# Half-group input projections with 512-row products, and the time mixing's gate projected ahead of the keys

## The chip, the cores and the metric

The kernel runs on one core of a Trainium2 chip. The metric is the device time of one execution in microseconds (us). TensorE (PE) multiplies matrices into PSUM; VectorE (DVE), ScalarE (ACT) and GpSimd (POOL) work on tiles in SBUF and PSUM; SyncE (SP) issues most of the loads. Each engine runs its own list of instructions in order, and waits where an instruction needs a result that is not there yet.

## What is computed

Two decoder layers over 256 tokens of width 2048. Each layer makes one input projection, gives its columns to three token mixers, gates each mixer's output, joins the three and projects them back:

```python
for l in range(DEPTH):
    u = x @ w_in[l]
    (cb, cc, ch, cg, cq, ckv, kpe, mg, rcols, rg) = _split(u, IN_SIZES)
    y_conv = _short_conv_branch(cb, cc, ch, cg, conv_w[l])
    y_mla = _mla_branch(cq, ckv, kpe, mg, ...)
    y_rwkv = _rwkv7_branch(rcols, rg, ...)
    mix = jnp.concatenate([y_conv, y_mla, y_rwkv], axis=-1)
    x = _layer_norm(DEEPNORM_ALPHA * x + mix @ w_out[l], ln_g[l], ln_b[l])
```

The convolution branch is `cb * conv3(cc * ch) * silu(cg)`. The attention branch norms `cq` and `ckv`, projects queries from the one and keys and values from the other, attends with 8 heads, and multiplies with `silu(mg)`. The time mixing (RWKV-7) runs a recurrence over the tokens with 8 heads of 64, norms its output by head (a group norm), adds a bonus term, and multiplies with `silu(rg)`.

## The kernel before

All products keep full precision by splitting both factors in a high and a low part (float32r): `hi` is a rounded copy made on ScalarE, `lo` the rest, made by a subtraction on VectorE (`split_in`). A product of two such factors is three TensorE products (`mm3`, lines 331 to 334): high by high, high by low, low by high.

The input projection is done in 12 groups of 512 columns. `in_group` computes one: for each of 16 blocks of 128 of the 2048 input rows, and each of 4 blocks of 128 columns, `mm3` multiplies a 128x128 block of weights with the 256 tokens of x. That makes 64 triples of 256-row products a group. The result lies in two accumulators of one PSUM bank each (`u_NAME_0`, `u_NAME_1`; pool `pp`, 4 buffers), and the work behind reads it there. Weights come as loads of 1 MB on SP's queue (`load`, three buffers in pool `wr`, asked for one load ahead by `LOOK`), and are split on ScalarE and VectorE in steps of 1024 columns into `hi_NAME` and `lo_NAME` (four buffers each).

The order of the groups is k, r, a, v, cq, cc, ch, cb, cg (`MAIN`), then the keys and values (`mla_kv`, products pkn and pvt in four rounds) and queries (`mla_q`, pqn and pqp) of the attention, and then rg, mg0, mg1 (`LATE`). rg is the gate of the time mixing, mg0 and mg1 are the gates of the attention.

The other work of a layer is written as generators (`rwkv`, `latent`, `conv`) that are advanced by `tick()` between the groups' steps. The order of each engine's list is then set by a scheduler, which weighs priorities (`tc.high_priority`) and when it believes each instruction can start.

The time mixing works in four chunks of 64 tokens. `pg` holds products within a chunk, made of `ar` and of `bk`; half of `bk` is written by POOL (lines 565 and 572). `bd`, `bt`, `xi` and the steps `tm` invert a triangular matrix on VectorE; `xd` and `xq` are moves of the result through DMA, and `pz` and `px` finish it. Then comes the serial part. For each chunk c, `prh_c` applies the state to the chunk's inputs, `rhs` adds `qs`, `pu_c` multiplies by the inverse and is copied to `uvt` (one half on VectorE, one on ScalarE), `pst_c` and two VectorE operations make the next state `st_c`, and after every second chunk `py_0`, `py_1` give the output. `py` is copied to `y`, normed by head (`gm`, `gsq`, `gv`, `grs` and the small steps `nr_g`), turned by `pt` into `yy`, and with the bonus `bon` and the gate (`th_rg`) becomes `mr`, a factor of the output projection. `mc` is that of the convolution, and `ma0`, `ma1` those of the attention.

The keys and values leave PSUM by copies of ScalarE into `kn` and `vt`, and a split into `vs`. These tiles, like `mc`, `mr`, `ma` and others, take turns in slots of the pool `sl`. The output projection (`out_proj`, products po) uses 512-row products, with the weights as the moving factor.

Of the kernel before, what the change touches and what calls it, by code (L numbers as in the profile page):

```python
# [10 lines left out]
F32 = mybir.dt.float32  # L11
# [13 lines left out]
AHEAD = 1500  # L25
GATE = 'V'
OFF = 2
LOOK = 1
# [3 lines left out]
N8 = 9  # L32
HEADS = 8
# [50 lines left out]
def lay_out(inp):  # L84
# [3 lines left out]
    w = inp["w_in"][:, :, idx].reshape(L, NKC, P, len(GROUPS), 512)  # L88
    o = {"x": inp["x"], "positions": inp["positions"]}
    o["xT"] = inp["x"][0].T.reshape(NKC, P, S).transpose(1, 0, 2)  # L90
    o["w_in"] = w.transpose(0, 3, 2, 1, 4)
# [18 lines left out]
def hybrid_layers(ctx: ExitStack, tc: tile.TileContext, x, positions, xT, w_in, w_out, w_uq, w_ukv, par, wa_in, gb_in,  # L110
# [189 lines left out]
    def split_w(raw, name, behind, to):  # L300
        nk, n = raw.shape[1:]
        k = 1024 // n if n == 256 else 2
        hi, lo = to or [wh.tile([P, k, 1024 // k], F32R, tag=t, name=f"{t}_{name}") for t in ("hi", "lo")]
        with tc.high_priority(AHEAD):
            ops = split_in(hi[:, 0:nk, 0:n], lo[:, 0:nk, 0:n], raw)
# [36 lines left out]
    MAIN, LATE, ORDER = ("k", "r", "a", "v", "cq", "cc", "ch", "cb", "cg"), ("rg", "mg0", "mg1"), (0, 12, 4, 8)  # L342

    def plan():

        for l in range(L):
            for names in (MAIN, None, LATE):
                if names is None:
                    yield from ((f"ukv{l}_{i}", 0, 2, w_ukv[l, i]) for i in range(4))
                    yield from ((f"uq{l}_{i}", 0, 4, w_uq[l, i]) for i in range(4))  # L350
                for name in names or ():
                    first = l == 0 and name == GROUPS[0]
                    for k0, nk in STEPS if first else [(k, 4) for k in (0, 4, 8, 12)]:
                        yield f"{name}{l}", k0, nk, w_in[l, GROUPS.index(name)]
            for g in range(3):
                yield from ((f"wo{l}_{g}", k0, 4, w_out[l, g]) for k0 in ORDER)
# [3 lines left out]
    loads, ready, asked = plan(), {}, []  # L360

    def load():
# [4 lines left out]
        n = src.shape[2]  # L367
        raw = to = behind = None
        if name == "k0":
            load_x(k0, nk)  # L370
            raw = s4(f"w_first{k0}", (P, nk, 512)) if k0 < 10 else None
        elif name[0] == "k":
            behind = mark.get(int(name[1])) if k0 else None
        elif name == f"wo{L - 1}_3_0" or name[0] == "w" and name[2] != str(L - 1) and name[3:] == "_3_1" and k0:
            s = s8(f"wl{name}_{k0}", (P, 2, 4, 256), F32R)
            to = s[:, 0], s[:, 1]
        if raw is None:
            raw = wr.tile([P, 4, n] if n < 512 else [P, 4, 512], F32, tag="raw", name=f"w_{name}_{k0}")
        i = nc.sync.dma_start(raw[:, 0:nk], src[:, k0:k0 + nk, :])
        if not params:  # L380
            in_turn(1, i)
        d = 4 if n == 256 else 2
        ready[name, k0] = [(k0 + k, split_w(raw[:, k:min(k + d, nk)], f"{name}_{k0}_{k}",
                                            behind and k0 + k > 2 and behind[k0 + k > 4], to))
                           for k in range(0, nk, d)]
# [6 lines left out]

    def in_group(l, xs, name):
        ps = [pp.tile([P, 2, S], F32, tag="acc", name=f"u_{name}{l}_{i}") for i in range(2)]
        first = l == 0 and name == GROUPS[0]
        if first:
            warm_up()
        for k0, step in STEPS if first else [(k, 4) for k in (0, 4, 8, 12)]:
            for k2, (hi, lo) in weights(f"{name}{l}", k0):
                for kc in range(k2, min(k2 + 2, k0 + step)):  # L400
                    k = kc - k2
                    for b in range(4):
                        mm3(ps[b // 2][:, b % 2, :], hi[:, k, b * P:(b + 1) * P], lo[:, k, b * P:(b + 1) * P],
                            *hl(xs, kc), kc == 0 and b % 2 == 0, kc == NKC - 1)
# [944 lines left out]
```

## Time and profile before

| | |
|---|---|
| median of 3 runs | 933.12 us (930.76 to 933.73) |
| profiled execution | 930.57 us |
| its span, first to last instruction | 928.8 us |
| granted TensorE clock, mean | 0.996 |
| products on TensorE | 7719 |

The profile lists how long each engine was busy, and how often an engine stood idle and whose result ended that. Views used below are the page of the whole execution; the waits of an engine (total, times, longest); the timeline (start and duration of each instruction, in us from the start of the span); the groups of instructions by tile (least, median and longest duration in ns, first and last start); and windows, which give for each stretch its length and the busy time and number of instructions of PE, PEld (weight loads), DVE, ACT and POOL, then the granted TensorE clock, the DMA share and GB/s. Where products follow each other on TensorE, the distance of their starts is the time that they take; the durations in the rows are longer, since products overlap.

### The profile page before, as it was taken

How to read it: one execution, taken by the hardware profiler on the slowest of the kernel's cores; microseconds unless marked ns; L12 is line 12 of the kernel's file. 1: busy time of each engine (PE TensorE's matmuls, PEld its weight loads, DVE VectorE, ACT ScalarE, POOL GpSimd, SP SyncE). 2: the span in 40 equal slices, each digit the busy share in tenths (PEclk: the TensorE clock that was granted, in tenths of full speed). 3: DMA queues.
4: the chain of work that ended last, by engine and by line, in shares of the span. 5: the costliest groups of instructions: out<-in, count | busy, mean ns of one | idle time of the engine just before them, and what ended most of it. 6: DMA issues, size and time to landing. Idle time of an engine off the chain costs nothing.

```text
span 928.8 us, 18409 instructions
## 1 busy us (share of the span) xinstructions
PE 910.0 (98%) x7719; PEld 867.6 (93%) x7719; DVE 682.1 (73%) x1132; ACT 468.2 (50%) x716; POOL 42.0 (5%) x47
## 2 busy tenths in 40 slices
PE   8999999999999999999999999999999999999996
PEld 7999989999989999888899999899998999998895
DVE  6687898886569875666766688988854898755665
ACT  6656535543455675434346465463434657754430
POOL 1210130000000000000010001300000000000000
PEclk9999999999999999999999999999999999999999
DMA  8965355354425435964665544463544363259542
GB/s 295 288 200 181 137 187 165 127 183 137 163 98 188 176 127 170 345 208 149 204 227 182 178 148 175 148 203 136 183 117 137 135 225 141 97 175 371 177 136 90
DMA packets 47523, 165.12 MB, mean 178 GB/s; under 512 B 13446, under 2 KB 22198, under 8 KB 32582
## 3 DMA queue, kind: packets, MB, share of 16 engines
q1 hardware_dynamic: 39680, 150.35, 47.4%
q10 hardware_dynamic: 5072, 9.57, 3.3%
q0 software_dynamic: 2688, 4.03, 1.6%
q8 instruction: 60, 0.98, 0.4%
q14 instruction: 23, 0.19, 0.1%
HBM read 158.61 MB, written 5.32 MB: 177 GB/s over the span
## 4 chain that ended last, share of the span: by engine, by line
PE 89%; DMA 3%; DVE 3%; POOL 2%; ACT 1%; issue 1%; SPq 0%; DVEq 0%; ACTq 0%
PE po L332 6%; PE po L333 6%; PE po L334 6%; PE u_mg L334 3%; PE u_mg L333 3%; PE u_mg L332 3%; PE u_ch L332 2%; PE u_cg L333 2%; PE u_cc L332 2%; PE u_cg L332 2%; POOL bk L572 2%; PE u_cg L334 2%; PE u_rg L334 2%; PE u_rg L333 2%; PE u_rg L332 2%; PE u_cb L334 2%
## 5 line engine op out<-in xcount | busy, mean ns | idle before, releaser
L136 DVE TENSOR_TENSOR lo_wo<-w_wo,hi_wo 128x1024 fp32r<-128x1024 f32 x57 | 69.4, 1223 | 51.7 <-ACT hi_wo L136 50.3
L136 ACT CAST hi_wo<-w_wo 128x1024 fp32r<-128x1024 f32 x57 | 59.8, 1053 | 80.8 <-PE po L334 56.0
L333 PE MATMUL u_mg<-x,hi_mg 128*128 128x256 f32 x256 | 72.6, 283 | 0.0
L334 PE MATMUL u_mg<-x,lo_mg 128*128 128x256 f32 x256 | 72.6, 283 | 0.0
L332 PE MATMUL u_mg<-x,hi_mg 128*128 128x256 f32 x256 | 72.4, 283 | 0.0
L136 DVE TENSOR_TENSOR lo_mg<-w_mg,hi_mg 128x1024 fp32r<-128x1024 f32 x32 | 39.1, 1223 | 18.5 <-ACT hi_mg L136 18.4
L333 PEld LDWEIGHTS u_mg<-x,hi_mg 128*128 128x128 f32 x256 | 49.1, 192 | 0.0
L334 PEld LDWEIGHTS u_mg<-x,lo_mg 128*128 128x128 f32 x256 | 49.0, 192 | 0.0
L332 PEld LDWEIGHTS u_mg<-x,hi_mg 128*128 128x128 f32 x256 | 49.0, 192 | 0.0
L333 PE MATMUL po<-lo_wo,ma 128*128 128x512 f32 (+1 forms) x128 | 46.4, 362 | 0.0
L334 PE MATMUL po<-hi_wo,ma 128*128 128x512 f32 (+1 forms) x128 | 46.4, 362 | 0.0
L332 PE MATMUL po<-hi_wo,ma 128*128 128x512 f32 (+1 forms) x128 | 45.9, 363 | 0.0
L136 ACT CAST hi_mg<-w_mg 128x1024 fp32r<-128x1024 f32 x32 | 33.6, 1049 | 22.1 <-PE u_mg L333 13.3
L332 PE MATMUL u_ch<-x,hi_ch 128*128 128x256 f32 x128 | 37.0, 289 | 0.0
L333 PE MATMUL u_cg<-x,hi_cg 128*128 128x256 f32 x128 | 37.0, 289 | 0.0
L334 PE MATMUL u_cq<-x,lo_cq 128*128 128x256 f32 x128 | 37.0, 289 | 0.0
L332 PE MATMUL u_k<-x,hi_k 128*128 128x256 f32 x128 | 36.5, 290 | 0.4 <-ACT hi_k L136 0.3
L333 PE MATMUL u_cq<-x,hi_cq 128*128 128x256 f32 x128 | 36.7, 287 | 0.0
L332 PE MATMUL u_cc<-x,hi_cc 128*128 128x256 f32 x128 | 36.7, 289 | 0.0
L332 PE MATMUL u_cq<-x,hi_cq 128*128 128x256 f32 x128 | 36.6, 286 | 0.0
L332 PE MATMUL u_cg<-x,hi_cg 128*128 128x256 f32 x128 | 36.6, 286 | 0.0
L334 PE MATMUL u_k<-x,lo_k 128*128 128x256 f32 x128 | 35.6, 285 | 0.9 <-DVE lo_k L136 0.9
(424 smaller groups left out, 3417.2 us busy)
## 6 DMA issues: line engine op xcount, KB each, us to landing
w_wo<-in_w_out_dram SPq DMA_DIRECT2D x24, 1024.0 KB, 6.1
w_mg<-in_w_in_dram SPq DMA_DIRECT2D x16, 1024.0 KB, 4.8
w_r<-in_w_in_dram SPq DMA_DIRECT2D x8, 1024.0 KB, 6.4
w_a<-in_w_in_dram SPq DMA_DIRECT2D x8, 1024.0 KB, 4.9
w_v<-in_w_in_dram SPq DMA_DIRECT2D x8, 1024.0 KB, 4.9
w_cq<-in_w_in_dram SPq DMA_DIRECT2D x8, 1024.0 KB, 4.8
w_cc<-in_w_in_dram SPq DMA_DIRECT2D x8, 1024.0 KB, 4.9
w_ch<-in_w_in_dram SPq DMA_DIRECT2D x8, 1024.0 KB, 5.2
```

Of the source, the lines that this page charges most:

```text
L136: inst = call(*args, **kwargs)
L332: m = T.matmul(o, lh, rh, start=first, stop=False, skip_group_check=True)
L333: T.matmul(o, lh, rl, start=False, stop=False, skip_group_check=True)
L334: T.matmul(o, ll, rh, start=False, stop=last, skip_group_check=True)
L572: G.tensor_tensor(bk[hi_, :, 64:128], c16(kkn)[hi_], c16(pinv)[hi_], ALU.mult)
```

## The change

Five things change together.

1. All groups but k are computed in two half-groups of 256 columns. One product of a weights' high part with 512 rows (x high and x low side by side) replaces two products of 256, and one product of the low part with x high follows. The two halves of the sums lie side by side in an accumulator of two banks (`acc`, 2 buffers instead of 4 of one bank). On the way out ScalarE copies the one half to SBUF and VectorE adds the other, into `u2_NAME` (in the instruction lists printed as `u_NAME`, with a number), or into `ccc`, `ccq`, `ckv` for the groups whose copies in SBUF were made separately before. k keeps its three 256-row products (`wide_group`).
2. Loads are of 0.5 MB instead of 1 MB, five buffers of half the size, asked for two ahead.
3. rg moves from `LATE` to the end of `MAIN`, ahead of keys and queries. The tiles of keys and values of a round share one accumulator (`pkv`), those of the queries too (`pq`), and their way out has a higher priority (`EVICT`).
4. POOL's two passes over `bk` become eight chunks, and `pg` of a chunk waits for its own chunks alone.
5. The first product of several small steps is given all the waits of the step (`gather`), and their two halves are taken in the other order.

```diff
-LOOK = 1
+EVICT = 4000
+LOOK = 2
...
-    pp = ctx.enter_context(tc.tile_pool(name="pp", bufs=4, space=PSUM))
+    pp = ctx.enter_context(tc.tile_pool(name="pp", bufs=2, space=PSUM))
...
-    wr = ctx.enter_context(tc.tile_pool(name="wr", bufs=3))
+    wr = ctx.enter_context(tc.tile_pool(name="wr", bufs=5))
...
+    def gather(m, earlier):
+
+        for e in earlier:
+            after(m, e)
...
-    MAIN, LATE, ORDER = ("k", "r", "a", "v", "cq", "cc", "ch", "cb", "cg"), ("rg", "mg0", "mg1"), (0, 12, 4, 8)
+    MAIN, LATE, ORDER = ("k", "r", "a", "v", "cq", "cc", "ch", "cb", "cg", "rg"), ("mg0", "mg1"), (0, 12, 4, 8)
+
+    def acc(name):
+
+        return pp.tile([P, 2, 512], F32, tag="acc", name=name)
...
+        whole = c4(f"c{name}{l}") if name in ("cc", "cq") else None
+        pairs = []
+        for i in range(2):
+            ps = acc(f"u_{name}{l}_{i}")
+            for k0 in range(0, NKC, 4):
+                _, (hi, lo) = weights(f"{name}{l}_{i}", k0)
+                for k in range(4):
+                    x2 = xs[k0 // 4][:, :, k, :]
+                    for b in range(2):
+                        c = slice(b * P, b * P + P)
+                        T.matmul(ps[:, b, :].rearrange("p (i t) -> p i t", i=2), hi[:, k, c], x2, start=k0 + k == 0,
+                                 stop=False, skip_group_check=True)
+                        T.matmul(ps[:, b, 0:S], lo[:, k, c], x2[:, 0, :], start=False, stop=k0 + k == NKC - 1,
+                                 skip_group_check=True)
...
+            with tc.high_priority(AHEAD):
+                A.copy(to, ps[:, :, S:2 * S])
+                V.tensor_tensor(to, to, ps[:, :, 0:S], ALU.add)
...
-        G.tensor_tensor(bk[hi_, :, 64:128], c16(kkn)[hi_], c16(pinv)[hi_], ALU.mult)
+        ready_ = []
+        for c in range(4):
+            if c == 2:
+                chunk(3, kp, 0)
+            ready_.append([chunk(c, kkn, 64)])
...
-            pk = pp.tile([P, 2, S], F32, tag="acc", name=f"pkn{l}_{h2}")
-            pv = pp.tile([P, 2, S], F32, tag="acc", name=f"pvt{l}_{h2}")
+            pk, pv = (t.rearrange("p (b c) -> p b c", b=2) for t in (lambda a: (a[:, 0], a[:, 1]))(acc(f"pkv{l}_{h2}")))
...
-            with tc.high_priority(AHEAD):
+            with tc.high_priority(EVICT):
```

TensorE's list at the end of layer 0's recurrence, before the change; names as above, with buffer numbers behind them. First the place of pu_2, then that of pst_2:

```order
1942 L333 MATMUL pkn_3_3250<-hkv_1647,hi_ukv_3_0_0_3203 128x256
1943 L334 MATMUL pkn_3_3250<-hkv_1647,lo_ukv_3_0_0_3204 128x256
1944 L774 MATMUL pu_2_2921<-rhs_2_2885,xq_2409 64x64 x8
1945 L332 MATMUL pvt_3_3251<-hi_ukv_3_0_0_3203,hkv_1647 128x256
1946 L333 MATMUL pvt_3_3251<-lo_ukv_3_0_0_3204,hkv_1647 128x256
```

Large products of keys and values (12 of pvt_3) stand between pu_2 and pst_2; 19 of pqn_0 follow prh_3 in the same way, and pt comes only in the group mg0. After the change, at the same step:

```order
1519 L338 MATMUL pkv_1_2986<-lo_ukv_1_0_2895,hkv_1434 128x256
1520 L339 MATMUL pkv_1_2986<-hi_ukv_1_0_2894,hkv_1434 128x256
1521 L843 MATMUL pu_2_2531<-rhs_2_2506,xq_2091 64x64 x8
1522 L859 MATMUL pst_2_2564<-uvt_1678,bkt_1609 64x64 x8
1523 L836 MATMUL prh_3_2598<-st_2_2573,ar_1156 64x64 x8
1524 L843 MATMUL pu_3_2634<-rhs_3_2607,xq_2091 64x64 x8
1525 L812 MATMUL py_1_0_2645<-uvt_1678,gs_1_1290 64x64 x8
```

The steps of the last two chunks stand one behind the other. A little further on, where py_1 ends:

```order
1542 L821 MATMUL py_1_1_2646<-st_1_2441,ar_1156 64x64
1543 L821 MATMUL py_1_1_2646<-st_2_2573,ar_1156 64x64
1544 L902 MATMUL pt_0_2809<-cs,y_2318 128x128 x4
1545 L902 MATMUL pt_1_2840<-cs,y_2318 128x128 x4
1546 L337 MATMUL pkv_2_3021<-hkv_1434,hi_ukv_2_0_2941 128x256
```

pt follows py_1 directly, and the third round of keys follows pt. ScalarE's list, before the change, where the keys leave PSUM:

```order
158 L136 COPY uvt_1928<-pu_1_2767 64x4x64
159 L136 CAST hi_uq_0_0_2_3246<-w_uq_0_0_3240 128x2x384
160 L136 COPY kn_3097<-pkn_0_3106 128x512
161 L136 COPY kn_3097<-pkn_1_3153 128x512
162 L136 COPY y_2671<-py_0_0_2824 128x4x64
163 L136 COPY y_2671<-py_0_1_2825 128x4x64
164 L136 COPY kn_3097<-pkn_2_3207 128x512
```

and after it:

```order
186 L138 COPY y_2318<-py_1_1_2646 128x4x64
187 L138 ACTIVATE gsq_2712<-y_2318 128x1024
188 L138 ACTIVATE yy_2808<-pt_0_2809,pars 128x256 x2
189 L138 ACTIVATE yy_2808<-pt_1_2840,pars 128x256 x2
190 L138 CAST mr_2917<-yy_2808 128x512
191 L138 COPY kn_2936<-pkv_0_2945 128x512
192 L138 CAST vs_2938<-pkv_0_2945 128x256
193 L138 COPY kn_2936<-pkv_1_2986 128x512
194 L138 CAST vs_2938<-pkv_1_2986 128x256
195 L138 CAST mr_2917<-yy_2808 128x512
196 L138 COPY vt_2937<-pkv_0_2945 128x256
```

The first copy of keys now stands behind the group norm's square, the four pieces of yy and the first half of mr. VectorE's list after the change, between the groups cc and ch:

```order
154 L138 TENSOR_TENSOR bon_1535<-pb_0_1536,vx_1463 128x512
155 L138 TENSOR_TENSOR bon_1535<-pb_1_1568,vx_1463 128x512
156 L138 TENSOR_TENSOR lo_ch_0_12_1756<-w_ch_0_12_1753,hi_ch_0_12_1755 128x1024
157 L138 TENSOR_TENSOR hkv_1434<-ckv_833,hkv_1434 128x512
158 L138 TENSOR_SCALAR nv_q_1505<-prsq_1498 128x256
159 L138 TENSOR_TENSOR ccc_1358<-ccc_1358,u_cc_0_1359 128x512
160 L138 TENSOR_TENSOR ccc_1358<-ccc_1358,u_cc_1_1512 128x512
```

Both halves of cc are added here one after the other; before the change the accumulators of cc were emptied by ScalarE's copies into `cu` alone.

More of the change, by code (lines that the diff above doesn't have):

```diff
@@ L32 @@
 N8 = 9
+NU = 3
 HEADS = 8
@@ L360, in hybrid_layers, with wide_steps @@
     loads, ready, asked = plan(), {}, []
+    def wide_steps(l):
+        return [(k, 2) for k in range(0, NKC, 2)] if l else STEPS
     def load():
@@ L374, in load @@
         elif name == f"wo{L - 1}_3_0" or name[0] == "w" and name[2] != str(L - 1) and name[3:] == "_3_1" and k0:
[L375 to L376 removed]
+            t = s8(f"wl{name}_{k0}", (P, 2, 4, 256), F32R)
+            to = t[:, 0], t[:, 1]
         if raw is None:
[L378 to L379 removed]
+            raw = wr.tile(shape, F32, tag="raw", name=f"w_{name}_{k0}")
+        i = nc.sync.dma_start(raw, src)
         if not params:
             in_turn(1, i)
[L382 to L385, printed above, removed]
+        ready[name, k0] = k0, split_w(raw, f"{name}_{k0}", behind and k0 > 2 and behind[k0 > 4], to)
     def weights(name, k0):
@@ L391, in weights, with wide_group @@
         return ready.pop((name, k0))
-    def in_group(l, xs, name):
[L394 to L404, printed above, removed]
+    def wide_group(l, xs, name):
+        ps = acc(f"u_{name}{l}")
+        if l == 0:
+            warm_up()
+        for k0, step in wide_steps(l):
+            _, (hi, lo) = weights(f"{name}{l}", k0)
+            for k in range(step):
+                for b in range(4):
+                    c = slice(b % 2 * P, b % 2 * P + P)
+                    mm3(ps[:, b // 2, b % 2 * S:b % 2 * S + S], hi[:, b // 2, k, c], lo[:, b // 2, k, c],
+                        *hl(xs, k0 + k), k0 + k == 0 and b % 2 == 0, k0 + k == NKC - 1)
+            used[0] += 1
+            if not (l == 0 and k0 < 2):
+                tick()
+        ps = [ps[:, i, :].rearrange("p (b t) -> p b t", b=2) for i in range(2)]
+        return [ps[b // 2][:, b % 2, :] for b in range(4)], ps
@@ L405, in in_group @@
                 used[0] += 1
-                if not (first and k0 < 2):
+                if k0 < 12:
                     tick()
-        return [ps[0][:, 0, :], ps[0][:, 1, :], ps[1][:, 0, :], ps[1][:, 1, :]], ps
+            if whole is not None:
+                to = whole[:, 2 * i:2 * i + 2, :]
+            elif (name, i) == ("a", 1):
+                to = c4(f"ckv{l}", (P, 2, S))
+            else:
+                to = sm.tile([P, 2, S], F32, tag="u2", name=f"u2_{name}{l}_{i}", bufs=NU)
@@ L564, in rwkv_scale, with chunk @@
         lo_, hi_ = halves
-        G.tensor_tensor(bk[hi_, :, 0:64], c16(kp)[hi_], c16(pinv)[hi_], ALU.mult)
+        bkc = bk.rearrange("p (b c) t -> p b c t", c=4)
+        def chunk(c, src, at):
+            cc = slice(c * 64, c * 64 + 64)
+            return G.tensor_tensor(bkc[hi_, :, c, at:at + 64], src[hi_, :, cc], pinv[hi_, :, cc], ALU.mult)
+        for c in range(3):
+            chunk(c, kp, 0)
         for b in range(4):
@@ L713, in rwkv_pairs @@
                     o = halves[1 - par]
-                    A.copy(hv(uvt, o, b2 * 2 + bb, par), pv[o, bb])
+                    st["uv1"] = A.copy(hv(uvt, o, b2 * 2 + bb, par), pv[o, bb])
             yield
@@ L772, in rwkv_chain @@
             for b in range(4):
-                for par in range(2):
-                    T.matmul(pu[rs[par], b, :], xq[rs[par], c, b, :], rhs[rs[par], b, :], start=True, stop=True)
+                for par in (1, 0):
+                    m = T.matmul(pu[rs[par], b, :], xq[rs[par], c, b, :], rhs[rs[par], b, :], start=True, stop=True)
+                    if c == b == 0 and par:
+                        gather(m, [st["xq1"]])
+            moved = []
             for par in range(2):
@@ L784, in rwkv_chain @@
                 for b in range(4):
-                    for par in range(2):
+                    for par in (1, 0):
                         h = 2 * b + par
-                        T.matmul(pst[rs[par], b, :], bkt[:, c, h, :], uvt[:, c, h, :], start=True, stop=True)
+                        m = T.matmul(pst[rs[par], b, :], bkt[:, c, h, :], uvt[:, c, h, :], start=True, stop=True)
+                        if b == 0 and par:
+                            gather(m, moved)
                 new = slot("st", f"st{l}_{c}", (P, 4, 64), 2)
@@ L1073, in conv @@
         yield from until(f"cc{l}")
-        x = c4(f"cu{l}")
-        with tc.high_priority(AHEAD):
-            for i in range(2):
-                A.copy(x[:, 2 * i:2 * i + 2, :], u["cc"][1][i])
+        x = u["cc"][2]
         yield from until(f"ch{l}")
```

127 lines of the change are left out of this document (72 added, 55 removed).

## The prediction

> **What bounds the kernel now.** I read the page's busy times and its chain first, then the waits of TensorE, then the timeline of its products, and last the stretch in which the recurrence ends.
>
> ```profile
> PE 910.0 (98%) x7719; PEld 867.6 (93%) x7719; DVE 682.1 (73%) x1132; ACT 468.2 (50%) x716; POOL 42.0 (5%) x47
> PE 89%; DMA 3%; DVE 3%; POOL 2%; ACT 1%; issue 1%; SPq 0%; DVEq 0%; ACTq 0%
> ```
>
> TensorE is busy for 98% of 928.8 us and is 89% of the chain that ended last: only fewer TensorE nanoseconds, or new waits on it, move the time. These are its two largest waits today (us in all, times, longest):
>
> ```profile
> PE prh L767 <- DVE st L136: 3.5, 2, 1.7
> PE pg L607 <- POOL bk L572: 2.7, 2, 1.4
> ```
>
> Little is waited for, because other work lies between the steps of the recurrence. The windows of its last part show it: keys and values from 243.7, queries from 263.5 us.
>
> ```profile
> 263.50:283.90 20.40, 20.38 (x224) 19.85 (x225) 16.16 (x30) 11.92 (x20) 0.40 (x1) 1.00 0.38 134
> 243.70:263.50 19.80, 17.91 (x242) 16.49 (x240) 10.72 (x20) 10.02 (x20) 0.00 (x0) 1.00 0.34 121
> ```
>
> Of these 40.2 us TensorE is idle for 1.9, while recurrence, group norm and keys all go on.
>
> The profiled execution took 930.57 us (span 928.8, 1.8 around it). The runs have a median of 933.12 and a spread of 930.76 to 933.73, about 0.3%, which is what a measurement can tell from no change. I sum against 930.57 and shift by 2.5 us at the end.
>
> **Part 1, pairs for triples.** The 256-row products start 0.12 us apart, the 512-row ones 0.227 us (0.68 for three):
>
> ```profile
> 259.92 0.28 PE L332 MATMUL pvt<-hi_ukv,hkv 128*128 128x256 f32 x1
> 260.04 0.28 PE L333 MATMUL pvt<-lo_ukv,hkv 128*128 128x256 f32 x1
> 260.16 0.28 PE L334 MATMUL pvt<-hi_ukv,hkv 128*128 128x256 f32 x1
> 260.37 0.34 PE L787 MATMUL pst<-uvt,bkt 128*64 128x64 f32 x4
> 400.05 0.39 PE L334 MATMUL po<-hi_wo,mr 128*128 128x512 f32 x1
> 400.27 0.39 PE L332 MATMUL po<-hi_wo,mr 128*128 128x512 f32 x1
> 400.50 0.39 PE L333 MATMUL po<-lo_wo,mr 128*128 128x512 f32 x1
> 400.73 0.39 PE L334 MATMUL po<-hi_wo,mr 128*128 128x512 f32 x1
> ```
>
> So 256 more rows cost 0.1067 us and a product has 0.0133 us of its own. Three products take 0.360, the pair 0.3467. Two layers of 11 groups (all but the keys' k) of 64 triples are 1408: 1408 x 0.0133 = **-18.8 us**. The same rows also bound it: nothing in them makes a pair cheaper than its 768 rows (0.320, -56 us in all) or dearer than the triple (0). A second part: the orders hold 162 changes between large and small products today and 106 after. The last row of a group above lasts 0.21 instead of 0.12 (260.16 to 260.37): 56 x 0.09 = **-5.0** (0 if the merged steps wait instead).
>
> **Part 2, adding the halves.** 44 half-groups each get a copy on ScalarE and an add on VectorE; rows of the same forms:
>
> ```profile
> L136 ACT COPY cu<-u_cc x4: 578/582/587, 161.8 to 621.7; 128x512 f32<-128x512 f32 x4
> L136 DVE TENSOR_TENSOR cu<-u_ch,cu x4: 674/675/676, 191.1 to 650.0; 128x512 f32<-128x512 f32 x4
> ```
>
> That is 44 x 0.58 = 26 and 44 x 0.675 = 30 us, less about 6 for the copies that go (cu, cq, ckv). It lies beside TensorE, on engines 50% and 73% busy, and costs 0 wherever the other accumulator is free for 11 us. The cover is missing at one place: the adds of u_cc stand behind both bon, a lo split, hkv and nv_q (0.69, 0.69, 1.2, 0.69, 0.42, then 0.68 itself: 4.4, estimated by the rows of their shapes here), both accumulators are u_cc's till then, and TensorE has only about 4 us of small products to do after the one that bon needs half a microsecond in. 1 us each layer, **+2.0** (0 to 10, if VectorE comes late).
>
> **Part 3, the gate ahead of the keys.** This is the large term. After pkv_1 the order holds pu_2, pst_2, prh_3, pu_3, py_1, pt, and only then pkv_2; today two dozen large products, and later a whole group, lie between these. With two accumulators, pkv_2 needs pkv_0's, and ScalarE reads that (kn, vs, vt) behind yy and mr, which need pt, which needs the whole norm. So TensorE sits through a chain that it now hides. Its rows (ns: least, median, most):
>
> ```profile
> L136 DVE COPY uvt<-pu x8: 416/417/417, 235.3 to 725.5; 64x256 f32<-64x256 f32 x8
> L136 ACT COPY uvt<-pu x8: 367/368/368, 235.8 to 725.9; 64x256 f32<-64x256 f32 x8
> L136 DVE TENSOR_TENSOR rhs<-prh,qs x6: 412/417/424, 243.8 to 722.3; 128x256 f32<-128x256 f32 x6
> L136 ACT COPY y<-py x8: 376/388/403, 253.0 to 731.7; 128x256 f32<-128x256 f32 x8
> L136 DVE TENSOR_REDUCE gm<-y x2: 1210/1210/1211, 274.2 to 732.7; 128x16 f32<-128x1024 f32 x2
> L136 DVE TENSOR_TENSOR y<-y,gm x2: 1225/1225/1225, 278.6 to 737.1; 128x1024 f32<-128x1024 f32 x2
> L136 ACT ACTIVATE gsq<-y x2: 1061/1062/1062, 280.0 to 738.4; 128x1024 f32<-128x1024 f32 x2
> L136 DVE TENSOR_REDUCE gv<-gsq x2: 1220/1220/1220, 284.4 to 742.8; 128x16 f32<-128x1024 f32 x2
> 302.01 0.17 DVE L136 SCALAR_TENSOR_TENSOR grs<-nr_g,grs 128x16 f32<-128x16 f32 x1
> 302.21 0.17 DVE L136 TENSOR_TENSOR nr_g<-grs 128x16 f32<-128x16 f32 x1
> L136 DVE TENSOR_TENSOR y<-y,grs x2: 1218/1218/1219, 303.9 to 762.3; 128x1024 f32<-128x1024 f32 x2
> L136 ACT ACTIVATE yy<-pt,pars x8: 557/566/576, 308.5 to 768.1; 128x256 f32<-128x256 f32 x8
> L136 DVE TENSOR_TENSOR yy<-yy,bon x4: 689/690/691, 310.4 to 769.9; 128x512 f32<-128x512 f32 x4
> L136 DVE SCALAR_TENSOR_TENSOR yy<-sg_rg,yy x4: 687/688/690, 313.0 to 772.3; 128x512 f32<-128x512 f32 x4
> L136 ACT CAST mr<-yy x4: 605/606/606, 314.4 to 774.1; 128x512 fp32r<-128x512 f32 x4
> L136 ACT COPY kn<-pkn x8: 586/587/592, 252.1 to 716.4; 128x512 f32<-128x512 f32 x8
> L136 ACT CAST vs<-pvt x8: 373/384/403, 261.4 to 720.5; 128x256 fp32r<-128x256 f32 x8
> L136 ACT COPY vt<-pvt x8: 372/372/374, 263.1 to 722.4; 128x256 f32<-128x256 f32 x8
> ```
>
> - Recurrence steps that lose their cover (the wait on st is paid today already): pu_2 to pst_2 and pu_3 to py_1, 0.42 + 0.37 each, prh_3 to pu_3 0.42, with hand-overs of some 0.1: 2.2 us.
> - Norm: two y copies 0.78, gm 1.21 and its scale 0.2, the subtraction 1.22, gsq 1.06, gv 1.22, eleven steps on 128x16 at 0.205 (302.01 to 302.21) 2.26, the last product 1.22, six hand-overs 0.6: 9.8 us.
> - pt to pkv_2: two yy 1.1, bon 0.69, gate 0.69, then ScalarE in order mr, kn, vs, kn, vs, mr, vt = 0.61 + 0.59 + 0.38 + 0.59 + 0.38 + 0.61 + 0.37 = 3.5, hand-overs 0.4, less pt_1's own 0.45 on TensorE: 5.9 us.
>
> 17.9 a layer, both layers in the same order: **+35.8**. Neighbouring instructions overlap by some 0.1, so 15 is the lower end, 20 the upper. After it pkv_3 and the queries find their accumulators free. Nothing here can be negative: the order is fixed and TensorE has nothing else in it.
>
> The clock after such waits, by the column before the last two:
>
> ```profile
> 126.00:129.00 3.00, 1.63 (x17) 1.31 (x18) 2.98 (x2) 0.00 (x0) 1.69 (x1) 1.00 0.83 254
> 129.00:133.00 4.00, 4.00 (x29) 3.77 (x30) 2.13 (x4) 2.56 (x5) 0.00 (x0) 0.57 0.19 76
> 589.00:593.00 4.00, 4.00 (x49) 3.75 (x48) 2.71 (x5) 3.01 (x5) 0.00 (x0) 1.00 0.12 49
> ```
>
> After a wait of 1.4 us layer 0 lost 0.43 x 4 = 1.7 us to a granted clock of 0.57; layer 1, after the same wait, lost none. By these rows a wait costs 0 to 1.7; the new ones are far longer, so I take 1.7 a layer, **+3.4** (0 to 7). [...]
>
> **Part 4, the rest.** POOL's two passes become eight chunks, and pg starts after the first: the 2.7 us of waits could go, or grow (rival B). I take 0. Half-size loads are asked for two ahead, the same bytes; five buffers cover five steps of 2.8 us against the 3.5 us to landing of a load of that size:
>
> ```profile
> w_ukv<-in_w_ukv_dram SPq DMA_DIRECT2D x8, 512.0 KB, 3.5
> ```
>
> On SP's queue xd and xq now stand among the gate's loads instead of the keys', and their reader pz 41 products into u_cg's second half (7 us). Both 0, and 3.5 for each load that comes late. The last heads of the attention run inside the first output group, 29 products of 0.227 ahead of their reader, 6.6 us for a gate and a split of 0.7 each and two copies: 0.
>
> Sum: 930.6 - 18.8 - 5.0 + 2.0 + 35.8 + 3.4 = 948.0, 17.4 more. From the median: **950**.
>
> **The rivals.**
> A, faster: the weight loads, not the rows, set the 0.12 us (PEld is 93% busy), and a pair with one load less takes its bare 0.320. Then 948.0 - 37.5 = 910.5, 913 by the median. It decides from a pair of 0.334 on (17.4 / 1408 = 0.0124 below 0.3467). Against it: the 512-row products have twice the time for each load and the same 0.0133 on top. 0.08; with 0.02 for a pair near 0.334, no change.
> B, slower still: POOL. Passes of one shape took
>
> ```profile
> 109.86 2.78 POOL L565 TENSOR_TENSOR bk<-kp,pinv 64x1024 f32<-64x1024 f32 x1 [57.85 <-DVE kp L136]
> 119.68 8.02 POOL L572 TENSOR_TENSOR bk<-kkn,pinv 64x1024 f32<-64x1024 f32 x1 [7.04 <-DVE kkn L136]
> ```
>
> so POOL stood for 5.2 us while VectorE worked without a gap. pg's first product now stands in the 17th place of u_cc, ahead of VectorE work that waits for nothing (four lo splits, bk, four on rx, an add and three small ones: about 10 us by rows of such shapes); the chunk is issued some 4 us before TensorE comes to it, so if POOL gets in only behind that work, TensorE stands 6 us a layer: 962. Some chunks may find gaps, so 0.15. [...]
> C, slower still: VectorE, busier by 24 us net, brings u_cc's adds or its splits 4 us later than I count, twice: 958. It decides once VectorE passes the dense products, from 100% of a stage on; 0.10.
> D: a product that reads x in two pieces costs both pieces their 0.0133, and Part 1 saves nothing: 969. No row reads so; 0.03.
>
> **How the numbers follow.** My forecast 0.62, A 0.08 with 0.02 beside it, B 0.15, C 0.10, D 0.03. The forecast's own bounds (chain 15 to 20 a layer, clock 0 to 7, u_cc 0 to 4, changes -5 to 0) give 939 to 963; B and C carry the upper end to 968, and 934 leaves room for several terms at their lower bound at once. Faster 0.08, no change 0.02, slower 0.90.
>
> **What would show it.** TensorE idle for about 10 us before pt and 6 before pkv_2 in each layer, its waits naming y and vt (or the engine of them); pairs 0.347 apart, groups of 22 us; about 1 us before u_ch; TensorE's share below 94%. If the waits before pt and pkv_2 sum to less than 9 us a layer, or the pairs start 0.334 apart, the forecast is wrong.

## The result and the profile after

| | before | after |
|---|---|---|
| median of the runs, us | 932.4 (930.8 to 933.7) | 970.0 (967.9 to 970.5) |
| profiled execution, its span, us | 930.6, 928.8 | 970.5, 968.7 |
| mean granted TensorE clock | 0.996 | 0.964 |

The change makes the kernel slower: the ratio is 1.040 (1.038 to 1.042), +37.6 us. The forecast was +17.4 (950, range 934 to 968): right in sign, less than half of the size, and the time lies just outside the range.

The page of the changed kernel, in the two lines that were read first before:

```profile
PE 912.6 (94%) x6311; PEld 802.7 (83%) x6311; DVE 708.7 (73%) x1176; ACT 483.9 (50%) x750; POOL 47.6 (5%) x59
PE 78%; DVE 4%; ACT 2%; issue 1%; POOL 1%; DVEq 0%; ACTq 0%
```

TensorE is as long busy as before with 1,408 instructions fewer, and its share of the chain that ended last fell from 89% to 78%. Its waits (us in all, times, longest):

```profile
PE pt L902 <- DVE y L138: 19.0, 2, 9.6
PE pkv L337 <- ACT vt L138: 9.5, 2, 4.7
PE pg L663 <- POOL bk L614: 6.8, 2, 3.4
PE prh L836 <- DVE st L138: 2.2, 2, 1.1
```

The first two are the waits that the forecast named, in its size. The third was 2.7 before and had been forecast at no change. The end of layer 0's chain in four windows (TensorE's busy time is the second number, the granted clock the third from the end):

```profile
275.10:278.50 3.40, 2.48 (x43) 2.15 (x41) 1.28 (x2) 1.20 (x2) 0.00 (x0) 1.00 0.41 116
278.50:281.90 3.40, 1.70 (x38) 1.31 (x34) 1.59 (x4) 0.00 (x0) 0.00 (x0) 0.99 0.40 118
285.80:295.40 9.60, 0.30 (x6) 0.11 (x3) 7.00 (x17) 1.70 (x3) 0.00 (x0) 0.50 0.00 0
295.40:305.80 10.40, 5.63 (x25) 5.26 (x26) 4.73 (x8) 5.13 (x12) 0.00 (x0) 0.50 0.00 1
```

The clock falls to half at 281.9, four us ahead of the long wait, while TensorE still has small products, with idle gaps of up to 1.1 us between them; and it comes back only at 305.8, when dense products had run for 3.7 us. In all it stands at half for 64.9 us (without the kernel's last microseconds), where it was 3.4 before.

The pairs do what the forecast said. Rows of u_a in the timeline:

```profile
69.83 0.39 PE L437 MATMUL u_a<-x,hi_a 128*128 128x512 f32 x1
70.06 0.27 PE L439 MATMUL u_a<-x,lo_a 128*128 128x256 f32 x1
70.17 0.40 PE L437 MATMUL u_a<-x,hi_a 128*128 128x512 f32 x1
```

From pair to pair it is 0.34 to 0.35 us; the 64 pairs of the group take 22.2 us where the triples took 23.0. Not every group keeps this pace: in u_ch, u_cb and u_cg the pairs start 0.353 us apart on the mean, and 64 of them take 22.6 us.

**What the forecast had not looked at is VectorE ahead of the chain.** The product kkn times tha, which GpSimd's second half of bk waits for, and GpSimd's rows, before and after:

```profile
118.39 1.21 DVE L136 TENSOR_TENSOR kkn<-kkn,tha 128x1024 f32<-128x1024 f32 x1
```

```profile
127.15 1.21 DVE L138 TENSOR_TENSOR kkn<-kkn,tha 128x1024 f32<-128x1024 f32 x1
```

```profile
128.44 7.86 POOL L614 TENSOR_TENSOR bk<-kkn,pinv 64x256 f32<-64x256 f32 x4 [6.38 <-DVE kkn L138]
```

The query projection u_cq begins at 104.3 before and at 104.7 after, so the mixing's preparation is 8.4 us late against the projections. The delay leads back to the decay's small weights (tile wa, split into was). They are loaded by GpSimd's queue and split by ScalarE and VectorE, and the product pw needs them. Rows of the tile was, and of the load, before (nanoseconds, then the first and the last start; the first is layer 0's):

```profile
L499 POOL DMA_DIRECT2D wa<-in_wa_dram x4: 620/637/656, 23.7 to 359.0; - x4
L136 ACT CAST was<-wa x2: 1037/1042/1047, 39.4 to 466.4; 128x1024 fp32r<-128x1024 f32 x2
L523 PE MATMUL pw<-wah,was x8: 278/280/283, 85.7 to 549.9; 128*128 128x256 f32 x8
```

And after:

```profile
L544 POOL DMA_DIRECT2D wa<-in_wa_dram x4: 632/644/660, 49.1 to 497.3; - x4
L138 ACT CAST was<-wa x2: 1036/1036/1037, 85.9 to 562.4; 128x1024 fp32r<-128x1024 f32 x2
L568 PE MATMUL pw<-wah,was x8: 277/278/279, 91.0 to 572.4; 128*128 128x256 f32 x8
```

The load is issued 25 us later, behind others on GpSimd's queue. ScalarE's part of the split, which started 46 us ahead of pw before, now starts 5 us ahead of it, and VectorE's part ends at 88.9 instead of 77.5. u_v began at 79.4 and 80.6, so pw comes 10.4 us into it instead of 6.2. The rest of the delay gathers behind that, where VectorE also has the halves' adds and the splits of the weights to do. It goes on into the chain: the last masked block gs and the first product pz of the inverse, before

```profile
L136 DVE TENSOR_TENSOR gs<-pg,cs x8: 681/683/692, 129.5 to 141.9; 128x512 f32<-128x512 f32 x8
L673 PE MATMUL pz<-xt,gs x64: 191/191/212, 223.6 to 224.9; 32*32 32x32 f32 x64
```

and after

```profile
L138 DVE TENSOR_TENSOR gs<-pg,cs x8: 672/684/694, 139.4 to 155.5; 128x512 f32<-128x512 f32 x8
L733 PE MATMUL pz<-xt,gs x64: 191/191/212, 234.9 to 236.1; 32*32 32x32 f32 x64
```

The last gs starts 13.6 us later and pz 11.3 us. Between them VectorE's recurrence takes 53.7 us before and 55.3 after in this layer, from the first to the last of its 31 steps tm, and 53.7 and 59.0 in the other; it doesn't shorten when the projections do.

### The profile page after: what moved, and what is told of

It is laid out like the page before. It is cut to its first block, busy times and chain, and to the rows that moved or that the text cites. A ratio compares the mean times of both kernels' runs of the same rounds, so it can differ in the third digit from the quotient of the medians.

```text
span 968.7 us, 16007 instructions
## 1 busy us (share of the span) xinstructions
PE 912.6 (94%) x6311; PEld 802.7 (83%) x6311; DVE 708.7 (73%) x1176; ACT 483.9 (50%) x750; POOL 47.6 (5%) x59
## 4 chain that ended last, share of the span: by engine, by line
PE 78%; DVE 4%; ACT 2%; issue 1%; POOL 1%; DVEq 0%; ACTq 0%
PE u_mg L437 6%; PE po L337 6%; PE po L338 6%; PE po L339 6%; PE u_ch L437 3%; PE u_rg L437 3%; PE u_cg L437 3%; PE u_mg L439 3%; PE u_cb L437 3%; PE u_cc L437 3%; PE u_rg L439 2%; PE u_cc L439 2%; PE u_cg L439 2%; PE u_cb L439 2%; PE u_ch L439 2%; PE u_r L437 2%
## 5 line engine op out<-in xcount | busy, mean ns | idle before, releaser
L437 PE MATMUL u_mg<-x,hi_mg 128*128 128x512 f32 x256 | 90.4, 396 | 0.5 <-DVE rt_q L138 0.5
L437 PEld LDWEIGHTS u_mg<-x,hi_mg 128*128 128x128 f32 x256 | 48.0, 188 | 11.5 <-issue 0.8
L437 PE MATMUL u_cc<-x,hi_cc 128*128 128x512 f32 x128 | 48.4, 415 | 0.0
L437 PE MATMUL u_ch<-x,hi_ch 128*128 128x512 f32 x128 | 46.5, 405 | 0.0
L437 PE MATMUL u_r<-x,hi_r 128*128 128x512 f32 x128 | 45.5, 398 | 0.9 <-DVE kx L138 0.9
L437 PE MATMUL u_rg<-x,hi_rg 128*128 128x512 f32 x128 | 46.2, 402 | 0.0
L437 PE MATMUL u_cg<-x,hi_cg 128*128 128x512 f32 x128 | 45.5, 399 | 0.0
L437 PE MATMUL u_cb<-x,hi_cb 128*128 128x512 f32 x128 | 45.3, 399 | 0.0
L437 PE MATMUL u_v<-x,hi_v 128*128 128x512 f32 x128 | 44.9, 392 | 0.0
L437 PE MATMUL u_cq<-x,hi_cq 128*128 128x512 f32 x128 | 44.5, 391 | 0.0
L339 PE MATMUL u_k<-x,lo_k 128*128 128x256 f32 x128 | 37.6, 293 | 1.0 <-DVE lo_k L138 1.0
```

What stands on the lines that cost most here:

```text
L339: T.matmul(o, ll, rh, start=False, stop=last, skip_group_check=True)
L437: T.matmul(ps[:, b, :].rearrange("p (i t) -> p i t", i=2), hi[:, k, c], x2, start=k0 + k == 0, stop=False, skip_group_check=True)
```

## The experiments

Two theories went into them: the moved gate (the end of the chain has lost its cover and TensorE waits), and the half-groups (they cost by themselves, through buffers, adds and loads). Later a third came out of the trace, the late preparation. Medians of the runs are given, and the ratio to the kernel before, whose medians on the same chips were 930.9 to 932.0.

### 1. The gate behind the queries again, half-groups kept

```
-    MAIN, LATE, ORDER = (..., "cb", "cg", "rg"), ("mg0", "mg1"), ...
+    MAIN, LATE, ORDER = (..., "cb", "cg"), ("rg", "mg0", "mg1"), ...
```

> The changed kernel with one line put back: the time mixing's gate rg is projected behind the queries again, as in the kernel before; half-groups, products of 512 rows, loads and POOL's eight chunks stay. Theory of the moved gate: the changed kernel's waits of PE at the end of the chain (19.0 us for pt, 9.5 us for pkv) go, and with them about 4 us of waits between the chain's steps and some 10 us of lower clock around them: 970 - 43 = about 927 us, between 920 and 936. Theory of the half-groups (two accumulators of double size, more and smaller loads and the adds of the halves hold PE up wherever they stand): the time stays at 960 us or above.

945.1 us, ratio 1.013 (1.011 to 1.016): 25.0 less than the changed kernel, and 13.3 more than the kernel before, between the two theories. The two long waits are gone, but these are there (its waits of TensorE):

```profile
PE pg L663 <- POOL bk L614: 6.8, 2, 3.4
PE pst L859 <- ACT uvt L138: 6.4, 6, 1.4
PE prh L836 <- DVE st L138: 3.8, 4, 1.4
```

So the rest of the change, which by the price of Part 1 saves 18.7 us of products in this trace too, costs 32 elsewhere. The trace shows two places: the wait for GpSimd, and a chain whose last steps have the keys alone beside them (py ends at 273.5, the keys at 274.1).

### 2. The kernel before with the gate ahead of the keys

The same line, changed in the other direction in the kernel before.

> The kernel before with one line changed: rg is projected ahead of the keys, and nothing else (whole groups, triples of 256 rows, four accumulators). Theory of the moved gate: the end of the chain loses its cover here too; PE does two of the four keys' groups ahead of pt as in the changed kernel, so most of its 9.8 us and some of the 5.9 us a layer come, with 2 to 5 us a layer of clock: 932 + 23 = about 956 us, between 945 and 975. Theory of the half-groups: without them the move alone costs little, 932 to 938 us.

954.0 us, ratio 1.025 (1.022 to 1.027): +22.3, as the theory of the moved gate had it. Its waits show the same two in a smaller size:

```profile
PE pt L828 <- DVE y L136: 13.6, 2, 6.8
PE pkn L332 <- ACT kn L136: 5.8, 2, 2.9
```

Runs 1 and 2 part the change: the gate's place costs 22.3 (in the kernel before) to 25.0 (in the changed one), everything else 13.3 to 16.0. They don't part this rest: the half-groups, the smaller loads, the chunks and the gathered waits stand or go together in both.

### 3. The norm's transposes behind the keys

```
-        yield from until(f"rg{l}")
+        yield from until(f"uq{l}")
         yield from rwkv_gate(l, t, u["rg"][1])
...
         V.tensor_tensor(yf, yf, rs_.unsqueeze(2)..., ALU.mult)
-        yield
+        yield from until(f"uq{l}")
...
-        yield from until(f"chain{l}")
+        yield from until(f"uq{l}")
         m = t["mc"] = pair(f"mc{l}")
```

> The changed kernel, with its recording told to put the keys' and queries' work ahead of the transposes of the time mixing's output: the copies of the values and the norm's two transposes pt are recorded only once the queries are, so that PE has all of the keys (48 products of pkv, about 5 us) between the last py and pt. rg stays ahead of the keys. Theory of the moved gate (PE waits because nothing dense is left to lay beside the norm): the wait for y shrinks from 9.65 us a layer to about 4, that of pkv for the values' copies (5.15 us a layer) goes: 970 - 2 x 11 = about 948 us, between 940 and 956. Theory of the half-groups: the order at this place doesn't matter, 965 to 972 us.

953.5 us, 16.5 less than the changed kernel. The wait for y is no longer among its waits, but the one for the values, which was expected to go, stayed:

```profile
PE pkv L337 <- ACT vt L138: 9.4, 2, 4.7
PE pg L663 <- POOL bk L614: 6.8, 2, 3.4
```

Both accumulators are held by the first two groups of the keys, and ScalarE's copies of their values still stand behind the norm's square in its order. So taking the first wait away is worth 16.5 and not the 19.0 of its row, and keys and norm are tied by ScalarE's order too, not only by pt's place.

### 4. Unused products in the two long waits

```
+        busy(55, f"wa{l}", st["py1"])
...
+        busy(34, f"wb{l}", m)
...
+    def busy(n, name, earlier):
+        pz = pm.tile([P, 256], F32, tag="m", name=name)
+        for i in range(n):
+            m = T.matmul(pz, ones[:, 0:P], ones, start=True, stop=True)
+            if i == 0:
+                after(m, earlier)
```

> The changed kernel with unused products of 256 rows (ones by ones, into a buffer of its own) in PE's two long waits of each layer: 55 of them, about 6 us, while PE waits for the norm, and 34, about 3.6 us, while it waits for the values' copies. They need nothing and nobody reads them, so the waits stay as long as they were and only PE's idleness goes. If the lower clock around the waits costs time (23.9 and 27.3 us at half clock there, 281.9 to 305.8 and 759.7 to 787.0), the clock stays up and the products at its end run at full speed: 970 - 4 to 8 = about 964 us. If the clock costs nothing that ends the path: 970 us. If the unused products delay what they stand ahead of: above 972 us.

963.9 us, 6.1 less than the changed kernel, with 178 products more. The same stretch as above, in two windows of this run:

```profile
283.50:293.50 10.00, 8.51 (x69) 8.22 (x64) 6.99 (x17) 1.71 (x3) 0.00 (x0) 0.86 0.00 0
293.50:304.00 10.50, 9.42 (x79) 9.22 (x78) 5.15 (x9) 6.47 (x15) 0.00 (x0) 1.00 0.01 2
```

The clock is back at full ahead of pt, and stands at half for 20.5 us in all instead of 64.9 (mean granted clock 0.987 instead of 0.964). TensorE's other products stand in the same order as in the changed kernel, so about 6 us of the changed kernel are the clock's; 20.5 us at half are still in this run, and what they cost it doesn't show.

### 5. GpSimd's bk in two passes again

```
-        for c in range(3):
-            chunk(c, kp, 0)
+        G.tensor_tensor(bk[hi_, :, 0:64], c16(kp)[hi_], c16(pinv)[hi_], ALU.mult)
...
-        for c in range(4):
-            if c == 2:
-                chunk(3, kp, 0)
-            ready_.append([chunk(c, kkn, 64)])
+        last = G.tensor_tensor(bk[hi_, :, 64:128], c16(kkn)[hi_], c16(pinv)[hi_], ALU.mult)
+        ready_ = [[last] for c in range(4)]
```

> The changed kernel with GpSimd's bk made in two passes as in the kernel before, in place of eight chunks; all else stays. The recorded order then puts the first pg behind 41 products of u_cc instead of 17 (about 4 us later). Theory of the late preparation (VectorE finishes kkn times tha 8.8 us later against the same place of the query projection, 127.15 against 118.39 us, so GpSimd starts its second half late, 128.44 against 119.68, in whatever pieces): the wait of pg only changes its form, 3.78 us a layer less about 4 us of products and more at GpSimd's end: 964 to 971, about 968 us. [...]

961.2 us, 8.8 less, and 2.8 below the lower end of what was expected. The wait is nearly gone, since in the order the first pg moves behind 24 more products of u_cc:

```profile
PE pg L653 <- POOL bk L617: 1.7, 2, 0.9
```

From u_cc's first product to u_ch's it takes 36.4 us in both layers instead of 40.8 and 42.0, and the mean granted clock of the run is 0.969 instead of 0.964. So my reading that the wait would only change its form was wrong: GpSimd ends about as late against the projections (133.2, 30.7 us after u_cq's start, where the chunks end at 136.3, 31.6 us after it), but TensorE has work in front of it. The chunks, made so that pg can start early, put pg where its input was not yet there.

### 6. The small weights early, in the changed kernel

```
         yield from until(f"r{l}")
+        wa, ws = c4(f"wa{l}", (P, 2, 512)), c4(f"was{l}", (P, 2, 512), F32R)
+        ...
+        t["ws"] = ws
         yield from rwkv_r(l, pq, t, u["r"][0])
```

(the lines of the load and the split, moved from rwkv_decay as they are)

> The changed kernel with one thing moved: the load of the decay's small weights (wa) and their split (was) are recorded ahead of the time mixing's r in place of behind u_a, so that the products pw stand after 19 products of u_v in place of 60, and the first pg after 116 products of u_cq in place of 17 of u_cc. rg stays ahead of the keys, half-groups stay. Theory of the late preparation: pg's wait (3.78 us a layer, 1.65 before) and the half clock behind it shrink, 2 x 5 us, and the chain starts some 6 us earlier and has more products of rg and of the keys beside it, 2 x 1 to 2: 970 - 13 = about 957 us, between 952 and 963. Rival (GpSimd's chunks are what pg waits for, or the half-groups' adds on VectorE): the wait stays as it is, 966 to 972 us.

959.6 us, 10.4 less. The wait for GpSimd is no longer among its waits, with the chunks as they are: they end at 127.5, 20.2 us after u_cq's start. The product kkn times tha starts 13.1 us after it, where it was 22.5 in the changed kernel and 14.1 in the kernel before: the late weights account for the whole delay. A wait of u_r for VectorE's kx grew from 0.9 to 3.4 us. The waits of the gate's place stand as before:

```profile
PE pt L904 <- DVE y L138: 18.6, 2, 9.3
PE pkv L337 <- ACT vt L138: 9.4, 2, 4.7
```

Runs 5 and 6 take the same wait away from its two sides, the consumer's and the producer's. Run 6 does it with the eight chunks in place, so it isn't their number by itself that costs.

### 7. Both: the small weights early, the gate behind the queries

> The kernel with rg behind the queries (945 us) and the early small weights of the run before, together. Theory of the late preparation (what the half-groups cost beside their saving is that the mixing runs 8 to 11 us later than its cover): pg's wait and its clock go, 2 x 5 us, and part of the waits between the chain's steps beside the keys: about 933 us, between 927 and 939. Rival: 943 to 946 us.

929.7 us, ratio 0.9986 (0.9965 to 1.0007): the fastest of all, and not to be told from the kernel before. Against run 1 the early small weights are worth 15.3 us here. The tile was and the masked blocks in this run:

```profile
L138 ACT CAST was<-wa x2: 1037/1042/1046, 36.9 to 467.1; 128x1024 fp32r<-128x1024 f32 x2
L570 PE MATMUL pw<-wah,was x8: 278/282/285, 82.7 to 549.1; 128*128 128x256 f32 x8
```

```profile
L138 DVE TENSOR_TENSOR gs<-pg,cs x8: 669/670/674, 130.2 to 142.1; 128x512 f32<-128x512 f32 x8
```

pw comes 3.3 us into u_v and gs ends where it did before. With that the rest of the change costs no more than it saves, but no more is left of the 18.7 us than is lost elsewhere. The windows from the first product of the keys to the first of the gate rg show where; the kernel before, and then this run:

```profile
243.70:283.93 40.23, 38.32 (x466) 36.36 (x465) 26.91 (x49) 21.97 (x39) 0.40 (x1) 1.00 0.36 128
```

```profile
235.80:284.65 48.85, 42.59 (x514) 40.23 (x513) 31.11 (x59) 23.13 (x41) 0.79 (x2) 0.93 0.37 108
```

TensorE comes to the keys 7.9 us earlier, and takes 8.6 us longer from there to the gate, in which it is idle for 6.3 us instead of 1.9 and has a granted clock of 0.93 instead of 1.00.

### 8. Half of the gate ahead of the keys

The plan gets rg0 (columns of the first half) in MAIN and rg1 in LATE, pt is held until both are there, the small weights are early.

> A version made of what was learned: early small weights; the first half of rg (64 products, 11 us) ahead of the keys and its second half behind the queries; the norm's transposes pt recorded only after that second half. The chain has half of rg and two groups of the keys beside it, the norm has the keys and the queries. What stays: the two accumulators' copies of the values behind the norm's first steps (4.7 us a layer) and two or three waits of about 1 us between the chain's last steps. Theory: the kernel before, 932, less the half-groups' saving of 18.7, plus 2 x (4.7 + 3 + 3 of lower clock) = 934 us, between 922 and 945. If rg's place or the half-groups cost in another way than by missing cover, it stays above 950 us.

941.4 us, ratio 1.011 (1.008 to 1.013): within the expected range, but 7 above its middle and slower than run 7. The values' wait of run 3 is there again:

```profile
PE pkv L337 <- ACT vt L138: 9.4, 2, 4.7
```

### 9 to 11. A tenth 8 KB buffer for chain and keys

Chain and keys share nine buffers of 8 KB; a tenth lets the keys' copies go ahead before the chain ends.

```
-N8 = 9
+N8 = 10
...
-    wr = ctx.enter_context(tc.tile_pool(name="wr", bufs=5))
+    wr = ctx.enter_context(tc.tile_pool(name="wr", bufs=3))
```

on run 7 (9), on run 1 (10) and on the changed kernel (11):

> The kernel of 929.7 us (rg behind the queries, early small weights) with a tenth buffer of 8 KB for the tiles that the chain and the keys share, paid with two of the five landing buffers of the weights. In the order PE then has keys 2 and 3 and the first two groups of the queries between the chain's steps, since the two accumulators of the keys can be emptied before the chain ends. Theory of the missing cover: what the stretch of keys and queries costs over the kernel before in the 929.7 us (10.5 us a layer, 4.1 of it waits over 0.4 us and 1 to 3.5 lower clock) mostly goes: 929.7 - 2 x 6 to 9 = about 915 us, between 908 and 922. Rival (three landing buffers are too few, or the half-groups keep a cost of their own): 926 us or above.

> The kernel with rg behind the queries (945 us, the small weights where the changed kernel has them) with the tenth buffer, paid the same way. Theory: late preparation and missing buffer are two costs of their own; the waits between the chain's steps beside the keys go (REST of that kernel 15 us a layer over the kernel before), pg's wait stays: 945 - 2 x 6 to 9 = about 930 us, between 924 and 936. If the lateness alone made the chain fall outside its cover, the buffer does nothing: 942 to 947 us.

> The changed kernel with the tenth buffer alone (three landing buffers in place of five). rg stays ahead of the keys, and ScalarE's copies of the keys' first two groups still stand behind the norm and the gate in the order. Theory of the moved gate: the waits for the norm and for the values' copies (19.0 and 9.5 us) come from that order and stay: 965 to 972, about 969 us. Rival (the copies stand there only for want of a buffer): the second wait goes, 2 x 5 us and clock: about 957 us.

Run 9: 935.4 us, ratio 1.004 (1.003 to 1.006), 5.7 more than run 7, so its theory missed by 20 us. The waits of pst and prh shrank from 3.7 and 3.8 us to 1.8 and 1.1, but others stand in their place (that of u_r was 1.9 in run 7):

```profile
PE pq L337 <- DVE rt_q L138: 4.7, 2, 2.3
PE u_r L437 <- DVE kx L138: 2.9, 1, 2.9
PE po L338 <- DVE lo_wo L138: 2.4, 3, 0.9
```

The queries, now between the chain's steps, wait for the rotation that empties their accumulator, and with three landing buffers the output's weights come late. Run 10: 940.1 us, 4.9 less than run 1, between the ranges of its two theories, and its runs spread from 934.7 to 946.5; too little to decide. The wait for GpSimd, which was to stay, fell from 6.8 to 2.3 us. Run 11: 972.0 us, 2.0 more than the changed kernel, with the two long waits as they were, as expected, so they come from the order of the instructions and not from want of this buffer:

```profile
PE pt L902 <- DVE y L138: 18.7, 2, 9.3
PE pkv L337 <- ACT vt L138: 9.4, 2, 4.7
```

### 12. The tenth buffer paid otherwise

On run 7: N8 = 10, four landing buffers, NC4 = 4 in place of 5.

> The kernel of 929.7 us (rg behind the queries, early small weights) with the tenth 8 KB buffer, paid with one landing buffer of the weights (four stay) and one of the five 4 KB buffers that the convolution and the latent norms share. In the order the convolution's steps no longer stand between the steps of VectorE's recurrence, so that pz comes after 41 of cg's 128 products in place of 88, and the chain's steps have cg, all four keys and two groups of the queries beside them. Theory of the missing cover (the half-groups' saving is real, and is eaten because the chain, which runs at VectorE's pace, ends as late as before while its cover got shorter): the stretch of keys and queries costs about as much as in the kernel before, 929.7 - 2 x 6 to 9 = about 915 us, between 908 and 922. If the chain is not what holds the 929.7 us up, or four landing buffers are too few: 926 us or above.

933.7 us, ratio 1.003 (1.002 to 1.005), where 908 to 922 was expected. The convolution's steps left VectorE's recurrence. Its products, in this run

```profile
L138 DVE TENSOR_TENSOR tm<-bt,xi x31: 184/350/417, 161.8 to 210.7; 64x31 f32<-64x31 f32 x2, 64x60 f32<-64x60 f32 x2, 64x87 f32<-64x87 f32 x2, 64x112 f32<-64x112 f32 x2
```

and in run 7

```profile
L138 DVE TENSOR_TENSOR tm<-bt,xi x31: 175/350/417, 159.1 to 214.1; 64x31 f32<-64x31 f32 x2, 64x60 f32<-64x60 f32 x2, 64x87 f32<-64x87 f32 x2, 64x112 f32<-64x112 f32 x2
```

span 48.9 us instead of 55.0, each as long as before but with less between them, and pz came at 221.1 instead of 226.0. Yet the time did not fall. Ahead of u_v 3.4 us are lost, with a wait of u_r for kx of 3.2 us where run 7 has 1.9 (u_v begins at 82.8, in run 7 at 79.4). And TensorE waits for the queries' buffers:

```profile
PE pq L337 <- DVE rt_q L138: 4.7, 2, 2.4
PE pq L338 <- DVE lq L138: 2.5, 2, 1.2
```

## Why the prediction was right and wrong

The prediction had the direction and the main mechanism right, and two steps of it failed. The clock's term, +3.4, was mis-sized: it comes to about 15. And Part 4 put the wait for GpSimd at 0, where it comes to +4.3 and takes the clock with it, and the splits and loads at 0, where +3.6 stand. The second pace of the pairs, +5.7, was not in the sum at all.

The sum is redone with the starts of all rows of TensorE, after less before: the spacing of products beyond the price of Part 1 or the triples is put down to a wait (over 0.15 us from a large product, over 0.4 from a small one), to the half clock, or to the rest.

| term | forecast | measured |
|---|---|---|
| pairs for triples | -18.8 | -18.7 |
| pairs at a second pace, 0.353 us | 0 | +5.7 |
| changes between large and small | -5.0 | -2.2 |
| waits at the chain's end (Part 3), and the small ones of u_cc | +37.8 | +32.6 |
| wait for GpSimd (pg) | 0 | +4.3 |
| first group, u_r, output: late splits, loads and kx | 0 | +3.6 |
| lower clock | +3.4 | +15.0 |
| all | +17.4 | +40.3 |

(The last column is of the two profiled executions, 39.9 apart. It is an account, not a test: only for the waits at the chain's end, the wait for GpSimd and part of the clock is there a run that takes the cost away. The forecast's own bounds, 939 to 963, mix the profiled execution and the median; by the median they are 939 to 965.)

- **Part 1 was right for the fast pairs**, and with it rivals A and D are out: pairs at 0.347 are neither 0.320 nor 0.360. What it lacked is the second pace: u_a's 64 pairs take 22.2 us, u_cb's 22.6, so the pairs together save 13.0 us and not 18.8. And the changes brought less than half of the 5.0.
- **Part 2's hand-over was right in place, and its +2.0 is not seen.** The adds end at 167.67 and u_ch begins at 167.71, but the 5.7 us between the two groups hold more small products than the 4 us that were counted, and TensorE is busy for nearly all of it:

```profile
166.39 1.28 DVE L138 TENSOR_TENSOR ccc<-ccc,u_cc 128x512 f32<-128x512 f32 x2
162.00:167.70 5.70, 5.57 (x94) 4.65 (x92) 5.70 (x12) 5.49 (x15) 0.00 (x0) 1.00 0.79 204
```

- **Part 3 was right**: 9.65 and 5.15 us from py to pt and from pt to pkv in the trace (9.94 and 5.14 in the other layer), where 9.8 and 5.9 were forecast. The steps of the recurrence, forecast at 2.2 a layer, wait 5.6 us in all (prh, pst, pu), where it was 3.5 before. Run 2 shows the cause alone. That runs 2 and 1 give 22 to 25 us for it, and not 35.8 and the clock, has two sides: in run 2 the two waits are smaller (13.6 and 5.8 us), and in run 1 the gate no longer lies beside the chain's middle steps, which wait 12.3 us instead of 5.6.
- **The clock's term was mis-sized**, the largest miss: +3.4 (0 to 7) against about 15 in the account, of which run 4 shows about 6 by taking idleness away; the rest is not tested by itself. I had priced one fall per layer at 1.7 us; there are five falls in all, and two of them last 23.9 and 27.3 us: each reaches over the wait, the products after it and the next wait, and TensorE is busy for 9.6 and 12.9 us of it.
- **"I take 0" for GpSimd failed** (Part 4); "Both 0", for the loads and moves, is off by no more than the +3.6 of the table. The wait for GpSimd grew by 2.1 us a layer, and the clock fell with it for 3.4 and 6.8 us (before the change for 3.4 in one layer). The mechanism was not rival B's alone: GpSimd's second half took 7.86 us in chunks and 8.02 in one pass before, but its first chunk was issued at 128.44, 8.8 us later than before, for kkn came late. It is rival C in another place, VectorE (and ScalarE) late ahead of pg instead of at u_cc's adds. Runs 5, 6 and 7 give it 8.8, 10.4 and 15.3 us, more than the wait's own row. The mean granted clock of runs 5 and 6 is 0.969 and 0.967, where the changed kernel has 0.964; in run 7 the waits of pst take 3.7 us where run 1 has 6.4.

The mistake under the last point can be named: I followed each moved instruction from TensorE's side, and took the elementwise work ahead of it as being where it was. The change moved the load of the small weights behind others on GpSimd's queue without naming it. The kernel's text has it in the same place as before, so the new order of the lists did it; why the scheduler chose that order no run shows. The row of wa's load in the order of GpSimd would have given it away.

**What stays open**: with both causes undone (run 7) the 18.7 us are still not there at the end. Their account against the kernel before is -18.7 for the pairs, +6.8 for slower pairs, -2.6 for changes, +11.6 for waits (a good half of them between the chain's steps) and +2.6 for the clock. It fits that the serial part of the chain starts at VectorE's pace (pz at 226.0, 223.6 before) while the keys start 7.9 us earlier, so that what is saved ahead comes off its cover; but runs 9 and 12, made to give the cover back, found other waits in its place, and no run collects the saving. That the saving can be had is not shown. Nor does any run undo the smaller loads, the gathered waits, the new priority of the keys' way out or the scratch buffers of the tag b2 (two instead of three in the changed kernel) by themselves.

## What to carry to other kernels

Before a projection is moved, ask what lies beside the last serial stretch once it is gone; here a long chain of small steps was paid in 28.5 us of waits for y and vt, and again in the clock, which stood at half for 51.2 us around them. A faster dense part ahead of a chain that starts at another engine's pace saved nothing by itself here: what it gained by the start of the keys was lost beside the chain. And follow each side input of such a chain (here a load and a split of small weights) through its queue in the new order: in this kernel the load was issued at 49 us and the wait showed on TensorE at 130.

## What the runs showed of the hardware

In the profiles of the two kernels the half clock comes in stretches of 3.4 (three times), 6.8, 23.9 and 27.3 us, which are one, two, seven and eight times 3.41, but for the kernels' end. Ahead of each of the changed kernel's five falls TensorE was busy for 0.8 to 1.8 of the last 3.4 us (278.50 to 281.90 above: 1.70), and before its one fall the kernel before had 2.0. So none of the six came after 3.4 us that were wholly idle, and the one at 281.9 came after small products with idle gaps of up to 1.1 us, ahead of the long wait. But the busy time of such a stretch doesn't decide alone: in the kernel before one with 1.99 (719.72 to 723.13) has no fall behind it, and one with 2.05 (125.80 to 129.22) has. What sets the fall the runs don't settle.

Pairs of a 512-row and a 256-row product start 0.347 us apart in some groups (u_a, u_v, u_cq of layer 0) and 0.353 in others (u_ch, u_cb, u_cg), at a granted clock of 1.00 in both. In run 1 it differs for one group between the layers: 21.00 us within u_cb hold 123 products in the first and 121 in the second, both at 1.00. The 256-row triples of the kernel before show no such second pace (0.359 to 0.360 in every group), and no run tells what sets it.
